# Hybrid layer on one core: the last row tile's turning spread over gate/up blocks, the third key product placed nearer, two first down splits swapped, an own buffer for first parts

## The chip, the core and the metric

The kernel runs on one core of a Trainium2 chip. The metric is the device time of one execution in microseconds. The core has a matrix engine (PE), a vector engine (DVE), a scalar engine (ACT), a general engine (POOL) and a queue that issues most transfers (SP). Each engine runs its instructions in the order in which the program lists them for it.

## The reference, cut

One layer of a hybrid encoder: a gated DeltaNet and a short gated convolution side by side, an output projection, then a SwiGLU feed-forward. The input is 2048 rows of a new stream and 8 x 16 rows of running streams, 1024 columns each: 17 tiles of 128 rows.

```python
h = rmsnorm(x, g1);  P = h @ w_in                  # 1024 -> 3592 columns
qkv = silu(causal_dwconv(P[..., :1536]));  q, k = l2norm(q), l2norm(k)
A = where(i > j, (k * beta) @ k.T * decay, 0)      # in chunks of 64 rows
sol = triangular_solve(I + A, [v * beta, k * beta * exp(g)])
...                                                # state update over the chunks -> o
x = x + rmsnorm(concat(o, conv_out) @ w_o)         # output projection
h = rmsnorm(x, g2)
f = (silu(h @ w_gate) * (h @ w_up)) @ w_down       # 1024 -> 2816 -> 1024
x = x + rmsnorm(f)
```

All of it is in float32. The kernel splits each operand into a rounded high part and a low part (the remainder) and uses three products: high x high, high x low and low x high.

## The kernel before

The work runs in four phases on one core.

**Phase 1** (`tile_hybrid_layer_kernel`, to about L1160) projects the input and runs the DeltaNet. The 17 row tiles are in five groups (`GROUPS`) of 4, 4, 3, 3 and 3 tiles. For each group 28 blocks of 24 projection matmuls (L327) are run, in three slots of 9, 9 and 6. The order of PE here is written out by hand. Everything else that PE does for the group is hung into the slots by `plan()`: `PLAN` lists for each group the slot of every step, among them `pairs` (28 in groups 2 to 4: the products of the keys with themselves, `pair_keys`, L615 to L620), `load` (`solve_load`, L629: packing the result for the triangular solve), `store` (`solve_store`, L657: transposing the solution, L660 and L661) and `levels` (from `level_a`, L664, PE uses the solution, L672). Between `load` and `store` the solve runs in four pieces on DVE (L653, L655). `pair_keys` takes a bank of the two-bank pool `psg` (tile name `gbank`), and DVE multiplies it by the decay into AU (L620), which frees the bank. The decay itself has been scaled on DVE just before (`decay_scale`, L603). With three tiles the first two key products stand at slot `pairs`, the third at `pairs` + 3.

**Phase 2** is the output projection (`o_tile`): 48 matmuls for each row tile, then squares, a factor, and the rows. `o_rows` (L1244) computes the next norm's factor, scales the rows by it (hx, L1250, DVE), transposes them (ht, L1252, DVE) and stores them as hTd (L1255). For the last of the 17 tiles this is put off: `omark["last"]` holds it, and it runs after the first block of phase 3 (L1564).

**Phase 3** is gate/up (`gate_up`, L1494): three groups of 6, 6 and 5 row tiles, 22 blocks f each, of 84 matmuls (L1473). A block multiplies by a scheme with seven products in place of eight, so sums and differences of weight blocks are formed on DVE and POOL (L1439 to L1449), and copies on ACT (L1505 to L1507) empty PE's banks. During a group the rows of the next one are loaded (`ffn_load`, L1352) by `LOADF` from f = 4 on, into the pool `fd`, which is opened after the pools of phase 2 are closed (L1565).

**Phase 4** is the down projection in five chunks of the 2816 columns. `down_pair` (L1717) does seven products for a pair of row tiles; `load_parts` (L1650) loads the parts in the pieces (0, 2), (2, 4) and (4, 7), or (0, 4) and (4, 7) for the first two pairs of a chunk (`duo`), into a ring of three buffers named ar. `split` (L1641) rounds a part on ACT (L1644) and subtracts on DVE or POOL (L1647). The first parts of the first chunk are prepared during phase 3. `finish` (L1681) squares, scales and stores the rows in the last chunk.

Outside PE's order in phase 1, a planner fixes the order of each engine's instructions when the program is built, from a simulated run; `tc.issue_after` ties an instruction behind another one.

Of the kernel before, what the change touches and what calls it, by code (L numbers as in the profile page):

```python
# [9 lines left out]
F32 = mybir.dt.float32  # L10
# [37 lines left out]
TURNS = ({"k": ((19,), (19,), (31,), (31,)), "q": ((43,), (43,), (55,), (55,)), "v": ((52,), (52,), (64,), (64,))},  # L48
# [50 lines left out]
def kernel(  # L99
# [67 lines left out]
    with ExitStack() as ph:  # L167
# [723 lines left out]
        def plan(g, nx, events):  # L891
# [13 lines left out]
            for i in range(n):  # L905
                at(mask + i, decay_mask, g, i)
                at(pairs + 3 * (i // 2) + i % 2 - 1, decay_scale, g, i)
                at(pairs + 3 * (i // 2), pair_keys, g, i)
                at((52, 42, 33)[min(gi, 2)] + 3 * (i // 2), pair_queries, g, i)
# [303 lines left out]
        def o_tile(t, loads=()):  # L1213
# [20 lines left out]
            for n in range(2):  # L1234
                c = slice(n * 512, (n + 1) * 512)
                V.scalar_tensor_tensor(pss[n], pss[n], r, gpost[:, c], op0=ALU.mult, op1=ALU.mult)
                omark["V"] = V.tensor_add(xt[:, c], xt[:, c], pss[n])
            nc.scalar.dma_start(out=x2d[t], in_=xt)
            if t + 1 < NT:
                o_rows(t, xt, ss)  # L1240
            else:
                omark["last"] = lambda: o_rows(t, xt, ss)

        def o_rows(t, xt, ss):  # L1244
            for n in range(2):
                omark["A"] = A.activation(ojunk, xt[:, n * 512:(n + 1) * 512], AF.Square, accum_out=ss[:, 2 + n:3 + n])
            V.tensor_add(ss[:, 2:3], ss[:, 2:3], ss[:, 3:4])
            r = rstd(op, ss[:, 2:3], 1, 1.0 / D, EPS, "oy")
            hx = op.tile([P, D], F32, tag="hx", name="hx") if t else spare[0]
            V.tensor_scalar_mul(hx, xt, r)  # L1250
            ht = op.tile([P, D], F32, tag="ht", name="ht") if t else spare[1]
            V.transpose(ht, hx)  # L1252
            gi, i = FPLACE[t]
            if gi:
                nc.scalar.dma_start(out=hTd[gi][4 * i:4 * i + 4].rearrange("b f c -> (b f) c"), in_=ht)  # L1255
            for b in range(0 if gi else 4):
                c = i * P + 32 * b
                nc.sync.dma_start(out=hTd[gi][:, c:c + 32].rearrange("(j f) c -> f j c", f=32),
                                    in_=ht[32 * b:32 * b + 32].rearrange("f (j c) -> f j c", c=32))
# [79 lines left out]
    with ExitStack() as ph:  # L1339
# [218 lines left out]
        for gi in range(len(FGROUPS)):  # L1558
            if gi:
                *_, hid = ffn_prep(gi, hs, t3)  # L1560
            for f in range(NF):
                gate_up(gi, f, hid, gu_start(gi, f, hid))
                if (gi, f) == (0, 0):
                    omark["last"]()  # L1564
                    ps_o.close()  # L1565
                    fd = side.enter_context(tc.tile_pool(name="fd", bufs=1, reuse_waits="tile", side="right"))
                if f == 0 and gi + 1 < len(FGROUPS):
                    hs = {}
                    hload, loaded = ffn_load(gi + 1, fd, hs), []
                if gi + 1 < len(FGROUPS):  # L1570
                    with tc.issue_after(gmark["A"].ins):
                        while loaded:
                            ffn_gain(hs, [loaded.pop()])
# [35 lines left out]
    with ExitStack() as ph:  # L1609
# [40 lines left out]
        def load_parts(src, lo, hi, front=False):  # L1650
            n = src.shape[-2] * P
            a = da.tile([P, 4 * MC * P // 2], F32, tag="ar", name="ar", bufs=3)
            a = a[:, :(hi - lo) * n].rearrange("p (i c) -> p i c", c=n)
# [63 lines left out]
        def down_pair(ch, u, last):  # L1717
# [33 lines left out]
            for i in (0, 1, 2, 3, 5, 4, 6) if final else range(7):  # L1751
                b, mid, dst = steps[i]
                b = bank(b)
                if i == 3 and len(parts) == 4:
                    parts += load_parts(src, 4, 7)
                e = V if i in ((0,) if end else (0, 3)) or (duo and not ch and len(ready) < 2) else G
                if end and i == (4 if duo else 0):
# [190 lines left out]
```

## Time and profile before

| | us |
|---|---|
| median of 3 runs | 2416.18 |
| lowest, highest | 2414.71, 2419.66 |
| the profiled execution | 2417.77 |
| its span | 2415.7 |
| PE busy | 2398.2 |
| DVE busy | 1614.9 |
| ACT busy | 1065.4 |
| POOL busy | 564.0 |

The span is the time from the first to the last instruction of the profiled execution. "PE busy" is the time in which at least one matmul is running; span less PE busy is the time that PE waits, at the start, at the end and in between. DVE, ACT and POOL work beside PE, so their time counts only where PE has to wait for them.

### The profile page before, as it was taken

Reading aid. Unit: us, or ns where it says so; the run is one execution under the profiler, and the core shown is the slowest. Engines: PE = TensorE matmul, PEld = TensorE weight load, DVE = VectorE, ACT = ScalarE, POOL = GpSimd, SP = SyncE. Lnnn points to the kernel's source line nnn. Section 1 sums busy time; section 2 is a strip of 40 time slices with the busy share of each in tenths; the row PEclk is TensorE's granted clock in tenths of the full one; section 3 lists DMA queues with packets and bytes.
Section 4 is the critical chain, followed back from the end, with each engine's and each line's share of the span. In section 5 each row is a group of like instructions: output and inputs, shape, how many; then the busy total and the mean of one; then the engine's idle time right before and its main releaser. Section 6 shows DMA issues by size and latency. Waiting matters only on the chain.

```text
span 2415.7 us, 39069 instructions
## 1 busy us (share of the span) xinstructions
PE 2398.2 (99%) x14202; PEld 2200.6 (91%) x14202; DVE 1614.9 (67%) x3062; ACT 1065.4 (44%) x2367; POOL 564.0 (23%) x671
## 2 busy tenths in 40 slices
PE   9999999999999999999999999999999999999998
PEld 7888889999999988899999999999999988888877
DVE  7875765756767466888788744456455555676787
ACT  6645545546444444544444423334333345333443
POOL 1211001001110000255555100000000035455663
PEclk9999999999999999999999999999999999999999
DMA  8774655766787677698898888888988844334376
GB/s 296 253 244 170 221 199 195 256 218 238 259 262 256 226 186 232 216 345 286 278 278 265 288 253 255 255 266 270 304 301 285 249 155 131 100 117 129 118 234 207
DMA packets 317064, 561.37 MB, mean 232 GB/s; under 512 B 95940, under 2 KB 198536, under 8 KB 299592
## 3 DMA queue, kind: packets, MB, share of 16 engines
q1 hardware_dynamic: 216864, 490.66, 61.3%
q10 hardware_dynamic: 99784, 67.17, 8.9%
q8 instruction: 112, 1.84, 0.3%
q0 software_dynamic: 224, 1.05, 0.1%
q14 instruction: 80, 0.66, 0.1%
HBM read 400.09 MB, written 158.70 MB: 231 GB/s over the span
## 4 chain that ended last, share of the span: by engine, by line
PE 91%; DVE 4%; ACT 2%; DMA 1%; issue 1%; POOL 1%; ACTq 0%; SPq 0%; POOLq 0%; DVEq 0%
PE fbank L1473 35%; PE dbank L327 25%; PE fbank L1664 17%; PE dbank L1227 4%; PE ftbank L1227 4%; PE gbank L619 1%; PE tbank L385 1%; PE gbank L790 1%; PE gbank L806 1%; PE obank L798 1%; PE gbank L812 1%; PE obank L820 1%; PE gbank L626 1%; PE gbank L723 0%; PE gbank L501 0%
## 5 line engine op out<-in xcount | busy, mean ns | idle before, releaser
L1473 PE MATMUL fbank<-xh,fw 128*128 128x384 f32 (+1 forms) x3696 | 898.0, 326 | 2.9 <-ACT m L1506 1.7
L1473 PEld LDWEIGHTS fbank<-xh,fw 128*128 128x128 f32 x3696 | 651.0, 188 | 5.0 <-ACT m L1505 2.8
L327 PE MATMUL dbank<-hi,w 128*128 128x384 f32 (+1 forms) x2224 | 651.1, 363 | 0.0
L1473 PE MATMUL fbank<-xl,fw 128*128 128x384 f32 (+1 forms) x1848 | 601.9, 326 | 0.0
L327 PEld LDWEIGHTS dbank<-hi,w 128*128 128x128 f32 x2224 | 410.0, 188 | 40.2 <-issue 3.6
L1664 PE MATMUL fbank<-dw,as 128*128 128x512 f32 x1785 | 416.0, 391 | 2.7 <-ACT as L1644 1.3
L1664 PEld LDWEIGHTS fbank<-dw,as 128*128 128x128 f32 x1785 | 334.6, 188 | 77.1 <-ACT as L1644 1.7
L327 PE MATMUL dbank<-lo,w 128*128 128x384 f32 (+1 forms) x1112 | 396.6, 357 | 0.0
L1473 PEld LDWEIGHTS fbank<-xl,fw 128*128 128x128 f32 x1848 | 346.9, 188 | 0.0
L327 PEld LDWEIGHTS dbank<-lo,w 128*128 128x128 f32 x1112 | 209.3, 188 | 15.3
L1647 POOL TENSOR_TENSOR as<-ar,as 128x256 fp32r<-128x256 f32 (+1 forms) x202 | 173.8, 869 | 182.1 <-ACT as L1644 176.5
L1644 ACT CAST as<-ar 128x256 fp32r<-128x256 f32 (+1 forms) x287 | 118.9, 427 | 200.4 <-PE fbank L1664 144.4
L1617 DVE TENSOR_TENSOR acc<-acc,fbank 128x512 f32<-128x512 f32 x219 | 148.1, 683 | 87.3 <-PE fbank L1664 69.5
L1312 POOL TENSOR_TENSOR dw<-dr,dw 128x512 fp32r<-128x512 f32 x48 | 67.6, 1415 | 514.1 <-ACT dw L1310 513.8
L1448 ACT CAST fw<-rg 128x512 fp32r<-128x512 f32 x124 | 77.2, 622 | 224.5 <-PE fbank L1473 127.4
L331 DVE SCALAR_TENSOR_TENSOR acc<-R,vec,acc 128x512 f32<-128x512 f32 (+2 forms) x180 | 120.9, 673 | 27.8 <-ACT acc L368 22.4
L1521 DVE TENSOR_TENSOR c<-u,fbank 128x384 f32<-128x384 f32 (+1 forms) x66 | 34.8, 528 | 98.2 <-PE fbank L1473 98.2
L1517 DVE TENSOR_TENSOR m<-m,m 128x384 f32<-128x384 f32 (+1 forms) x44 | 23.1, 525 | 79.9 <-ACT m L1507 79.8
L1524 ACT ACTIVATE c<-c 128x384 f32<-128x384 f32 (+1 forms) x66 | 33.4, 507 | 95.3 <-DVE c L1523 95.3
L1449 POOL TENSOR_TENSOR fw<-rg,fw 128x512 fp32r<-128x512 f32 x44 | 66.6, 1515 | 34.7 <-ACT fw L1448 32.8
L1519 ACT ACTIVATE m<-fbank 128x384 f32<-128x384 f32 (+1 forms) x66 | 31.2, 473 | 94.4 <-PE fbank L1473 73.7
L360 POOL COPY hist<-R 128x3 f32<-128x3 f32 x60 | 18.5, 308 | 216.4 <-ACT R L336 171.6
(409 smaller groups left out, 3562.5 us busy)
## 6 DMA issues: line engine op xcount, KB each, us to landing
w<-wsplit SPq DMA_DIRECT2D x105, 1024.0 KB, 5.1
fw<-fsplit SPq DMA_DIRECT2D x188, 512.0 KB, 4.8
fsplit<-fw SPq DMA_DIRECT2D x94, 512.0 KB, 4.2
partd<-pt ACTq DMA_DIRECT2D x86, 384.0 KB, 6.5
rg<-in_w_gu SPq DMA_DIRECT2D x62, 512.0 KB, 4.3
wsplit<-w SPq DMA_DIRECT2D x28, 1024.0 KB, 4.9
ar<-partd SPq DMA_DIRECT2D x43, 384.0 KB, 3.2
wr<-in_w_in SPq DMA_DIRECT2D x32, 512.0 KB, 6.4
```

The source lines that it names most:

```text
L327: T.matmul(ps[:, :c], l[:, k, :], r[k][:, :c], start=(k == 0 and r is hi and l is wh), stop=(k == KD - 1 and l is wl))
L331: r = V.scalar_tensor_tensor(acc, raw(d), w[:, d:d + 1], acc, op0=ALU.mult, op1=ALU.add)
L1227: T.matmul(pss[n], m_[:, j, :], w_[k][:, n * 512:(n + 1) * 512], start=(k == 0 and ci == 0), stop=(k == KD - 1 and ci == 2))
L1312: e.tensor_tensor(out=w[1], in0=v, in1=w[0].bitcast(F32), op=ALU.subtract)
L1448: A.copy(w[:, 0], v)
L1449: e.tensor_tensor(out=w[:, 1], in0=v, in1=w[:, 0].bitcast(F32), op=ALU.subtract)
L1473: T.matmul(ps, w_[:, c], b_[k][:, :hw], start=(first and k == 0 and ci == 0), stop=(k == KH - 1 and ci == 2), skip_group_check=not first)
L1521: V.tensor_add(c21, u2, b3)
L1617: mark_d["V"] = V.tensor_tensor(out=dst if out is None else out, in0=dst, in1=ps, op=ALU.add)
L1644: ins = mark_d["A"] = A.copy(a[:, 0, :n], v)
L1647: mark_d["V" if e is V else "G"] = e.tensor_tensor(out=a[:, 1, :n], in0=v, in1=a[:, 0, :n].bitcast(F32), op=ALU.subtract)
L1664: ins = T.matmul(ps, a[:, x_, q * P:(q + 1) * P], w[y_], start=(start and q == 0 and ci == 0), stop=(q == c - 1 and ci == 2), skip_group_c ...
```

## The change

Four places are changed.

1. `o_rows` of the last row tile becomes a generator that is run in three steps after the blocks f = 0, 1 and 2 of gate/up. The squares and the factor stay at f = 0. The scaling hx moves from DVE to ACT, behind the last silu of block 1. The transposition on DVE comes behind the last product of block 2, with the store. The pools of phase 2 are closed, and fd is opened, at f = 2 in place of f = 0.
2. In the groups with three tiles the third key product moves from slot `pairs` + 3 to `pairs` + 1, its decay scaling from `pairs` + 2 to `pairs`, and `load` and `store` by two slots, from 32 to 30 and from 47 to 45.
3. In the first chunk of the down projection two subtractions change engines: pair 0's third one goes from POOL to DVE, pair 1's second one from DVE to POOL.
4. `load_parts` puts the loads of (0, 2) into a buffer of their own, af, in the pool `dn`; the ring ar serves the rest.

```diff
--- before.py
+++ after.py
@@ -42,9 +42,9 @@
 LATE = (*SEQS[0][:2], 7, 11, 19, 23, 27)
 PLAN = {0: (14, 20, 22, 26, 32, 36, 40, 50, (67, 69, 71), 75),
         1: (16, 20, 23, 28, 26, 33, 38, 51, (56, 58, 60), 66),
-        2: (8, 14, 17, 22, 17, 28, 32, 47, (52, 55, 58), 63),
-        3: (8, 14, 17, 22, 17, 28, 32, 47, (53, 56, 59), 64),
-        4: (8, 14, 17, 22, 17, 28, 32, 47, (52, 55, 57), 62)}
+        2: (8, 14, 17, 22, 17, 28, 30, 45, (52, 55, 58), 63),
+        3: (8, 14, 17, 22, 17, 28, 30, 45, (53, 56, 59), 64),
+        4: (8, 14, 17, 22, 17, 28, 30, 45, (52, 55, 57), 62)}
 TURNS = ({"k": ((19,), (19,), (31,), (31,)), "q": ((43,), (43,), (55,), (55,)), "v": ((52,), (52,), (64,), (64,))},
          {"k": ((17,), (20,), (23,), (26,)), "v": ((55,), (55,), (61,), (61,)), "q": ((62, 64), (63, 65), (64, 66), (65, 67))},
          {"k": ((14,), (14,), (17,), (17,)), "v": ((46,), (46,), (52,), (52,)), "q": ((57, 59), (58, 60), (59, 61), (60, 62))})
@@ -904,8 +904,8 @@
             at(norms, key_norms, g)
             for i in range(n):
                 at(mask + i, decay_mask, g, i)
-                at(pairs + 3 * (i // 2) + i % 2 - 1, decay_scale, g, i)
-                at(pairs + 3 * (i // 2), pair_keys, g, i)
+                at(pairs + (3 if n == MAXT else 1) * (i // 2) + i % 2 - 1, decay_scale, g, i)
+                at(pairs + (3 if n == MAXT else 1) * (i // 2), pair_keys, g, i)
                 at((52, 42, 33)[min(gi, 2)] + 3 * (i // 2), pair_queries, g, i)
             if gi:
                 at(QSUM[min(gi, 2)], query_sums, g)
@@ -1236,10 +1236,12 @@
                 V.scalar_tensor_tensor(pss[n], pss[n], r, gpost[:, c], op0=ALU.mult, op1=ALU.mult)
                 omark["V"] = V.tensor_add(xt[:, c], xt[:, c], pss[n])
             nc.scalar.dma_start(out=x2d[t], in_=xt)
+            rows = o_rows(t, xt, ss)
             if t + 1 < NT:
-                o_rows(t, xt, ss)
+                for _ in rows:
+                    pass
             else:
-                omark["last"] = lambda: o_rows(t, xt, ss)
+                omark["last"] = rows
 
         def o_rows(t, xt, ss):
             for n in range(2):
@@ -1247,9 +1249,16 @@
             V.tensor_add(ss[:, 2:3], ss[:, 2:3], ss[:, 3:4])
             r = rstd(op, ss[:, 2:3], 1, 1.0 / D, EPS, "oy")
             hx = op.tile([P, D], F32, tag="hx", name="hx") if t else spare[0]
-            V.tensor_scalar_mul(hx, xt, r)
+            yield
+            if t + 1 < NT:
+                V.tensor_scalar_mul(hx, xt, r)
+            else:
+                with tc.issue_after(gmark["A"].ins):
+                    A.activation(hx, xt, AF.Copy, scale=r)
+            yield
             ht = op.tile([P, D], F32, tag="ht", name="ht") if t else spare[1]
-            V.transpose(ht, hx)
+            with ExitStack() if t + 1 < NT else tc.issue_after(gmark["V"].ins):
+                V.transpose(ht, hx)
             gi, i = FPLACE[t]
             if gi:
                 nc.scalar.dma_start(out=hTd[gi][4 * i:4 * i + 4].rearrange("b f c -> (b f) c"), in_=ht)
@@ -1560,16 +1569,17 @@
                 *_, hid = ffn_prep(gi, hs, t3)
             for f in range(NF):
                 gate_up(gi, f, hid, gu_start(gi, f, hid))
-                if (gi, f) == (0, 0):
-                    omark["last"]()
+                if not gi and f < 3:
+                    next(omark["last"], None)
+                if (gi, f) == (0, 2):
                     ps_o.close()
                     fd = side.enter_context(tc.tile_pool(name="fd", bufs=1, reuse_waits="tile", side="right"))
-                if f == 0 and gi + 1 < len(FGROUPS):
+                if f == 2 and gi + 1 < len(FGROUPS):
                     hs = {}
                     hload, loaded = ffn_load(gi + 1, fd, hs), []
                 if gi + 1 < len(FGROUPS):
                     with tc.issue_after(gmark["A"].ins):
-                        while loaded:
+                        while f > 2 and loaded:
                             ffn_gain(hs, [loaded.pop()])
                     for _ in range(LOADF.count(f)):
                         k = next(hload)
@@ -1649,7 +1659,8 @@
 
         def load_parts(src, lo, hi, front=False):
             n = src.shape[-2] * P
-            a = da.tile([P, 4 * MC * P // 2], F32, tag="ar", name="ar", bufs=3)
+            a = (da.tile([P, 4 * MC * P // 2], F32, tag="ar", name="ar", bufs=3) if hi > 2 else
+                 dn.tile([P, 2 * MC * P // 2], F32, tag="af", name="af"))
             a = a[:, :(hi - lo) * n].rearrange("p (i c) -> p i c", c=n)
             (nc.gpsimd if front else nc.sync).dma_start(out=a, in_=src[:, lo:hi].rearrange("p i q c -> p i (q c)"))
             return [a[:, i] for i in range(hi - lo)]
@@ -1753,7 +1764,7 @@
                 b = bank(b)
                 if i == 3 and len(parts) == 4:
                     parts += load_parts(src, 4, 7)
-                e = V if i in ((0,) if end else (0, 3)) or (duo and not ch and len(ready) < 2) else G
+                e = V if i in ((0,) if end else (0, 3)) or (duo and not ch and (i > 1 if len(ready) < 2 else i == 2)) else G
                 if end and i == (4 if duo else 0):
                     load2()
                 if end and i == (5 if duo else 3):
```

## Rows read from the trace of the kernel before

**Rows 1.** The page's first part: busy us, share of the span, instructions.

```profile
PE 2398.2 (99%) x14202; PEld 2200.6 (91%) x14202; DVE 1614.9 (67%) x3062; ACT 1065.4 (44%) x2367; POOL 564.0 (23%) x671
```

**Rows 2.** Windows: start:end, length, busy by engine, PEclk, DMA share, GB/s.

```profile
1049.32:1063.78 14.46, 12.74 (x74) 12.42 (x73) 13.87 (x15) 5.75 (x12) 10.30 (x8) 1.00 1.02 405
2400.00:2416.00 16.00, 8.07 (x36) 6.36 (x34) 11.18 (x19) 2.90 (x8) 1.54 (x2) 0.90 0.38 119
```

**Rows 3.** Waits of PE: who <- for whom, us, times, longest.

```profile
PE fbank L1473 <- ACT m L1506: 1.7, 1, 1.7
...
PE fbank L1664 <- ACT as L1644: 1.3, 1, 1.3
...
PE fbank L1664 <- DVE as L1647: 1.0, 1, 1.0
PE gbank L672 <- DVE utd L660: 0.9, 1, 0.9
```

**Rows 4.** Timeline of DVE, gate/up: start, us, operation, [idle before].

```profile
1052.07 1.50 DVE L1250 TENSOR_SCALAR hx<-xo,oyr 128x1024 f32<-128x1024 f32 x1
...
1056.62 1.23 DVE L1252 STREAM_TRANSPOSE ht<-hx 128x1024 f32<-128x1024 f32 x1
...
1061.13 0.54 DVE L1523 TENSOR_TENSOR c<-u,fbank 128x384 f32<-128x384 f32 x1
...
1090.61 0.99 DVE L1449 TENSOR_TENSOR fw<-sD,fw 128x512 fp32r<-128x512 f32 x1 [1.16 <-ACT fw L1448]
```

**Rows 5.** Timeline of ACT there; last, all 128x1024 casts: total us, mean ns.

```profile
1061.70 0.52 ACT L1524 ACTIVATE c<-c 128x384 f32<-128x384 f32 x1 [2.23 <-DVE c L1523]
...
1062.90 0.48 ACT L1506 COPY m<-fbank 128x384 f32<-128x384 f32 x1 [0.17 <-DVE a L1537]
...
1072.76 0.62 ACT L1448 CAST fw<-sD 128x512 fp32r<-128x512 f32 x1 [1.49 <-PE fbank L1473]
...
L306 ACT CAST w<-wr 128x1024 fp32r<-128x1024 f32 x32 | 33.7, 1052 | 24.3 <-PE dbank L327 13.5 <-DMA wr<-in_w_in 10.5
```

**Rows 6.** Timelines of PE and DVE around the key products of group 3.

```profile
595.58 1.05 PE L619 MATMUL gbank<-kT 128*128 128x128 f32 x8
...
590.52 1.90 DVE L603 TENSOR_TENSOR dt<-dt,c 128x512 f32<-128x512 f32 x3 [2.34 <-ACT dt L599]
592.34 1.28 DVE L620 TENSOR_TENSOR AU<-gbank,dt 128x512 f32<-128x512 f32 x2
```

**Rows 7.** Timeline of PE where it takes up the solution of group 3.

```profile
631.72 0.69 PE L672 MATMUL gbank<-utd,AU 32*32 32x32 f32 x32 [0.89 <-DVE utd L660]
632.34 0.45 PE L327 MATMUL dbank<-hi,w 128*128 128x384 f32 x1
```

**Rows 8.** Timelines of POOL and DVE at the start of chunk 0.

```profile
1953.20 0.96 POOL L1647 TENSOR_TENSOR as<-ar,as 128x256 fp32r<-128x256 f32 x1 [10.53 <-ACT as L1644]
...
1955.94 4.14 DVE L1647 TENSOR_TENSOR as<-ar,as 128x256 fp32r<-128x256 f32 x4
```

**Rows 9.** All of line L1647: duration in ns, min/median/max, by engine.

```profile
L1647 POOL TENSOR_TENSOR as<-ar,as x202: 725/740/1477, 1953.2 to 2396.7; 128x256 fp32r<-128x256 f32 x77, 128x384 fp32r<-128x384 f32 x24
...
L1647 DVE TENSOR_TENSOR as<-ar,as x85: 409/420/1518, 1955.9 to 2382.3; 128x256 fp32r<-128x256 f32 x75, 128x384 fp32r<-128x384 f32 x10
```

**Rows 10.** Last chunk: timelines of ACT, DVE, SP, PE; a chain piece.

```profile
2309.68 0.52 ACT L1644 CAST as<-ar 128x384 fp32r<-128x384 f32 x1 [2.51 <-DMA ar<-partd]
...
2310.81 0.70 DVE L1696 TENSOR_TENSOR fbank<-fbank,gpo 128x512 f32<-128x512 f32 x1 [2.03 <-ACT junkd L1693]
...
2268.47 28.55 SPq L1654 DMA_DIRECT2D ar<-partd  x5
...
2306.08 6.54 SPq L1654 DMA_DIRECT2D ar<-partd  x4
...
2303.85 10.09 PE L1664 MATMUL fbank<-dw,as 128*128 128x512 f32 x43 [0.51 <-POOL as L1647]
...
2270.97 6.41 DMA ar<-partd
```

## The prediction

> **What bounds the kernel now.** I read the page first: PE is busy 2398.2 us, 99% of the span [rows 1]. The matmuls set the time, and the change removes no matmul, so whatever it can win is idle time of PE: 2415.7 − 2398.2 = 17.5 us. Second, the windows: in the last 16.0 us PE works 8.07, at a granted clock of 0.90 where the other stretch shown has 1.00 [rows 2]. That is 7.9 of the 17.5 us, and it lies in a tail that the diff does not touch. What is left, 9.6 us with the start, is in the list of PE's waits [rows 3], and the places that the diff names have four of its entries, and a fifth wait that a timeline shows [rows 10]:
>
> - 1.7 us, L1473 behind ACT's copy L1506: in the second gate/up block, before the copy's end at 1063.38
> - 0.9 us, L672 behind DVE's L660, the transposed solution of group 3: before 631.72
> - 1.0 us, L1664 behind DVE's low part L1647: chunk 0
> - 1.3 us, L1664 behind ACT's cast L1644, and 0.5 us, L1664 behind POOL's low part L1647: last chunk
>
> They add up to 5.4 us, 0.22% of the time, and that is the most which the four parts together can give. Third, the order in time on each engine around these places says what each wait hangs on.
>
> **Part 1, the last row tile.** In the second block DVE is busy for 13.87 of 14.46 us and PE for 12.74 [rows 2]: here DVE is the bound. DVE runs the scaling hx (L1250) at 1052.07 for 1.50 us and the transposition (L1252) at 1056.62 for 1.23, and only at 1061.13 the sum L1523 [rows 4]. ACT's silu L1524 waits 2.23 us for that sum, and the copy L1506 that lets PE go on ends at 1062.90 + 0.48 = 1063.38 [rows 5]; PE, 1.7 us idle, wanted it at 1061.7. The two operations are 2.73 us of DVE's time ahead of L1523, some 2.6 without the overlap of neighbours, so the copy can end near 1060.8, 0.9 us before PE wants it. The gap of 1.7 goes whole; what is late next is the same copy, with 0.9 to spare. Added elsewhere: the scaling on ACT, one pass over 128x1024. A cast of that shape takes ACT 1.05 us; twice as long would be 2.1. It stands behind the silu of the second block, and ACT has 1.49 us without work before 1072.76 [rows 5], so 1.05 is hidden and 2.1 would push the casts behind it by 0.6. I take the cast's 1.05, the nearest row. The transposition now follows L1537 of the third block, where DVE has 1.16 us idle before 1090.61 [rows 4] and needs 1.23: 0.1 late, within a block that has idle time. Its store moves with it on ACT's queue; the rows of this tile are read by loads of the last group, a group of 22 blocks later. The pool that takes the place of hx and ht opens two blocks later, but its first loads stand at the block with f = 4 as before, and SP keeps its order there: nothing. I take −1.7, bounds −1.9 and 0.
>
> **Part 2, the third key product.** Groups 2 to 4 have three tiles each. PE now does two key products, then 24 projection matmuls (9 + 9 + 6), then the third. The change leaves 6 between. 74 matmuls of the same width, 384, take 12.74 us in the second gate/up block [rows 2], 0.172 each, so the third product is wanted 18 x 0.172 = 3.1 us earlier, in group 3 at 595.58 − 3.1 = 592.5 [rows 6]. The solve then starts up to 3.1 us earlier and, as the place of L672 stays, group 3's wait of 0.9 goes. Groups 2 and 4 have no such wait and gain nothing.
>
> But the third product needs a bank. The pool has two, and both are held by the first two products until DVE has multiplied them by the decay (L620). DVE runs all three decay scalings (L603) first and then the two L620, which together take 1.28 from 592.34 [rows 6]; the first ends at about 593.0, and with some 0.06 for the signal PE would wait 593.06 − 592.48 = 0.6 us. The pattern is the same in groups 2 and 4: 3 x 0.6 = 1.8. That is one bound; the other is 0, if DVE takes the first L620 ahead of the second or third scaling. Nothing in the diff asks for that order, so I take 1.8. What queues behind the waiting product is all of PE, projections that need nothing of it. That PE lets nothing past shows at 631.72: L672 starts after 0.89 us of waiting, and matmuls of L327, which don't need it, come at 632.34 [rows 7]. The Trainium skill ("PSUM — Partial Sum Buffer", Engine vs sequencer instructions) states it as a rule: matmuls start and complete in program order. The trace agrees here; by that rule the early product costs PE its whole wait, and if others could pass it part 2 would be worth −0.9. Net: −0.9 + 1.8 = +0.9, bounds −0.9 and +1.8.
>
> **Part 3, the swap in chunk 0.** DVE is held by the last gate/up block and starts the low part of pair 1's second product at 1955.94; PE waits 1.0 us for it. POOL took pair 0's third low part at 1953.20 after 10.53 us without work [rows 8]. Swapped, POOL does pair 1's from about 1953.2 in 0.96, at most 1.48, the longest such row [rows 9]: by 1954.7, well before PE wants it at about 1956.5. DVE does pair 0's from 1955.94 in 0.42 to 1.52 [rows 9], done by 1957.5 at the worst; it belongs to the next product, and one product is six matmuls, 1.4 us at the rate of 43 in 10.09 us [rows 10], so it is wanted at about 1957.8. Some 0.3 to spare. I take −1.0, bounds −1.0 and −0.5.
>
> **Part 4, the first parts' own buffer.** In the last chunk ACT's cast at 2309.68 waited 2.51 us for a load into ar; a square stands behind it on ACT and holds DVE's gain L1696 at 2310.81 for 2.03 us [rows 10], and from there come the factor and the scaling that give PE a bank. SP issued that load at 2306.08 [rows 10], when a buffer of the ring came free, and it landed 3.6 us later. The load before it, of a pair's first parts, was issued at 2268.47 + 28.55 − 0.3 = 2296.7 [rows 10] and took the buffer that came free then. With the first parts out of the ring that buffer goes to the load in question, 9 us earlier, and the 1.3 goes. The 0.5 hangs on a chain that starts with the load of 6.41 us from 2270.97 [rows 10]; the loads ahead of it find their buffers earlier too, by some 1.5 us. −1.3 − 0.5 = −1.8, bounds −1.8 and 0 (0 if loads behind the new single buffer, on the same queue, come as late as now).
>
> **Sum.** −1.7 + 0.9 − 1.0 − 1.8 = −3.6 us. The profiled execution took 2417.77 and its span 2415.7; the same −3.6 on the median is 2416.18 − 3.6 = 2412.6. A measurement of this kernel can tell about 0.2%, 4.8 us, from no change, so the forecast is "within".
>
> **The rivals.** First: the wait for the bank does not arise, because DVE takes the first L620 ahead of a scaling. For it: the order is planned anew, and PE's third product now hangs on that one operation. Against: group 3 as it stands [rows 6]. All five gaps go: 2416.18 − 5.4 = 2410.8, just beyond 0.2%. Second: the waits change their place. DVE is busy 96% of the second block [rows 2], and one low part takes it 0.41 or 1.52 us [rows 9], so a fresh order can bring the wait back one operation later. If parts 1 and 4 give nothing, −1.0 + 0.9 is left: 2416.1. Third, the slower side: the solve of groups 2 to 4 is a chain of small DVE operations that comes up to 3.1 us earlier, ahead of work that drains PE's projection banks. There are three such banks, so nothing waits until that work is two products late, 2 x 24 x 0.172 = 8.3 us; from there each us by which the chain pushes it stops PE, at most 3.1 − 0.6 = 2.5 in a group, 7.5 in three: 2412.6 + 7.5 = 2420.1. Against it: none of the waits in [rows 3] is one of L327.
>
> **How the numbers follow.** The forecast has 0.41, the first rival 0.28, the second 0.23, the third 0.08. Faster by over 0.2% is the first rival, 0.28; slower is the third with what lies beyond, 0.08; within, the rest, 0.64. The range takes in the first rival with half a microsecond for its roundings and the second with the upper bound of part 2 (+0.9 more): 2410.2 to 2417.1.
>
> **What would show it.** In the list of PE's waits: no L1473 behind L1506 (part 1); no L672 behind L660, but three new entries of L619 behind DVE's L620 of some 0.6 each (part 2); no L1664 behind DVE (part 3), and none behind ACT or POOL (part 4). PE's idle time falls from 17.5 to about 14. The forecast is wrong if L619 waits nowhere (then near 2410.8), if new waits stand in the first blocks of gate/up, or if L327 waits in groups 2 to 4.

## The result and the profile after

The changed kernel takes 2420.87 us (median of 18 runs, 2417.5 to 2425.59) against 2416.36 of the kernel before (18 runs, 2414.69 to 2419.66). The ratio is 1.0019, with a 95% interval of 1.0011 to 1.0026: 4.5 us slower, where 3.6 us less were forecast. The runs also lie further apart, over 8 us in place of 5. The profiled execution took 2422.64 us (span 2420.8). That is 1.8 above the median, so its rows show a little more loss than a usual run has.

Lines from 1239 on have moved by up to 11: L1506 is now L1515, L1507 is L1516, L1523 is L1532, L1524 is L1533, L1449 is L1458, L1647 is L1657, L1664 is L1675. The page's first part, as in [rows 1]:

```profile
PE 2401.8 (99%) x14202; PEld 2202.6 (91%) x14202; DVE 1613.1 (67%) x3061; ACT 1066.7 (44%) x2368; POOL 562.7 (23%) x671
```

PE is busy for 3.6 us more with the same 14202 matmuls: besides waiting longer, it must have run slower somewhere. Its idle time, span less busy, is 19.0 us where it was 17.5; about 14 was forecast. The list of PE's waits, as in [rows 3]:

```profile
PE fbank L1675 <- DVE accs L1627: 2.5, 1, 2.5
PE fbank L1482 <- ACT m L1516: 2.1, 1, 2.1
...
PE gbank L619 <- DVE AU L620: 1.4, 3, 0.6
PE fbank L1482 <- ACT m L1514: 0.9, 3, 0.6
PE fbank L1675 <- POOL as L1657: 0.5, 1, 0.5
...
PE fbank L1675 <- DVE dw L1321: 0.4, 1, 0.4
...
PE fbank L1675 <- ACT as L1654: 0.3, 1, 0.3
```

L672 behind L660 is gone, L1664 behind DVE's low part is gone, and the 1.3 behind ACT's cast in the last chunk is gone. Three waits of L619 have come, as forecast. The 0.5 behind POOL's low part in the last chunk stays, though part 4 was to take it away. Two long waits were not forecast: 2.1 us in the second gate/up block, and 2.5 us near the end. (The 0.4 behind DVE's dw and the 0.3 behind ACT's cast, both in the first chunk, are new too.) Windows around the two long ones (start:end, length, busy by engine, PEclk, DMA share, GB/s):

```profile
1058.70:1060.70 2.00, 2.00 (x12) 1.71 (x10) 2.00 (x3) 0.00 (x0) 1.49 (x1) 1.00 1.05 412
1062.80:1066.00 3.20, 3.20 (x10) 3.20 (x11) 1.78 (x4) 1.78 (x4) 2.21 (x2) 0.50 0.90 294
1068.00:1072.00 4.00, 4.00 (x25) 4.00 (x24) 3.90 (x7) 2.35 (x4) 1.13 (x1) 1.00 0.32 131
2390.00:2394.00 4.00, 4.00 (x18) 2.96 (x16) 1.86 (x4) 2.33 (x6) 2.15 (x3) 1.00 0.38 89
...
2398.00:2400.00 2.00, 2.00 (x6) 1.61 (x5) 0.04 (x1) 0.04 (x1) 0.69 (x1) 0.50 0.52 141
2402.00:2404.00 2.00, 2.00 (x11) 1.63 (x10) 2.00 (x5) 0.20 (x2) 0.63 (x2) 1.00 0.71 262
```

Behind each of the two waits PE runs at half its clock, 1.2 in place of 2.4 GHz: in 3.2 us it begins 10 matmuls where 18 fit, and it is back at 1.00 by 1068. At the full clock 10 take 1.7 us, so this stretch cost 1.5 us beside the wait. Behind the wait of 2.5 us some eight matmuls begin 0.43 us apart in place of 0.23, which is 1.6 us. Together the two stretches are 3.1 of the 3.6 us by which PE is busier. In the kernel before, the waits of 1.7 and 1.3 us had no such stretch behind them: the granted clock there was 1.00.

The second block, DVE, then POOL and ACT (start, us, operation, [idle before]), where [rows 4, 5] showed the one of before:

```profile
1054.27 1.50 DVE L1458 TENSOR_TENSOR fw<-sC,fw 128x512 fp32r<-128x512 f32 x1
1055.69 1.78 DVE L1451 TENSOR_TENSOR sD<-rg,sB 128x512 f32<-128x512 f32 x1
1057.39 1.65 DVE L1545 TENSOR_TENSOR a<-c,m 128x384 f32<-128x384 f32 x1
1058.96 1.78 DVE L1458 TENSOR_TENSOR fw<-sB,fw 128x512 fp32r<-128x512 f32 x1
...
1061.27 0.54 DVE L1532 TENSOR_TENSOR c<-u,fbank 128x384 f32<-128x384 f32 x1
...
1055.18 1.74 POOL L1458 TENSOR_TENSOR fw<-sA,fw 128x512 fp32r<-128x512 f32 x1
1056.88 1.74 POOL L1458 TENSOR_TENSOR fw<-rg,fw 128x512 fp32r<-128x512 f32 x1
1058.58 1.61 POOL L1458 TENSOR_TENSOR fw<-ru,fw 128x512 fp32r<-128x512 f32 x1
...
1061.84 0.52 ACT L1533 ACTIVATE c<-c 128x384 f32<-128x384 f32 x1 [5.49 <-DVE c L1532]
...
1062.27 0.46 ACT L1516 COPY m<-fbank 128x384 f32<-128x384 f32 x1
```

The scaling and the transposition are gone from here, yet L1532 stands where L1523 stood, with a block that begins 0.8 us later on DVE (its first sA is at 1052.24 in place of 1051.47). The operations that moved up run beside POOL's three subtractions, and each takes about as long as one of those. And ACT waits 5.49 us in front of the silu L1533, with the copy L1516 that PE wants queued behind it. It is another copy than the one of before: L1516 was L1507, and in the kernel before ACT made that copy ahead of the silu:

```profile
1058.99 0.48 ACT L1507 COPY m<-fbank 128x384 f32<-128x384 f32 x1
```

So in the change PE stops one product of 12 matmuls earlier in its order than before. The copy that it then waits for ends at 1062.73, where the one of before ended at 1063.38, and PE wanted it at 1060.7 in place of 1061.7.

The end of the last chunk, on SP in the kernel before and, with DVE and PE, in the changed one:

```profile
2373.19 0.43 SPq L1654 DMA_DIRECT2D ar<-lastd  x1
...
2376.98 1.13 SPq L1654 DMA_DIRECT2D ar<-partd  x2
```

```profile
2372.40 0.38 SPq L1665 DMA_DIRECT2D af<-lastd  x1
...
2379.75 0.55 DVE L1657 TENSOR_TENSOR as<-af,as 128x384 fp32r<-128x384 f32 x1
...
2385.10 0.57 SPq L1665 DMA_DIRECT2D af<-partd  x1
...
2396.47 6.24 PE L1675 MATMUL fbank<-dw,as 128*128 128x512 f32 x19 [2.46 <-DVE accs L1627]
```

Before, the last pair's first parts were loaded 4 to 5 us after the single's parts (lastd). Now both use the one buffer af, and the load comes 12.7 us behind. DVE reads the single's parts out of af until 2380.30; the other 4.8 us pass on SP's queue, behind loads and stores of rows that wait themselves.

### The profile page after: what moved, and what is told of

Same layout as the page of the kernel before. It is cut to its first block, busy times and chain, and to the rows that moved or that the text cites. A ratio compares the mean times of both kernels' runs of the same rounds, so it can differ in the third digit from the quotient of the medians.

```text
span 2420.8 us, 39066 instructions
## 1 busy us (share of the span) xinstructions
PE 2401.8 (99%) x14202; PEld 2202.6 (91%) x14202; DVE 1613.1 (67%) x3061; ACT 1066.7 (44%) x2368; POOL 562.7 (23%) x671
## 3 DMA queue, kind: packets, MB, share of 16 engines
q0 software_dynamic: 224, 1.05, 0.1%
## 4 chain that ended last, share of the span: by engine, by line
PE 90%; DVE 4%; DMA 3%; ACT 2%; issue 1%; POOL 1%; SPq 0%; ACTq 0%; POOLq 0%; DVEq 0%
PE fbank L1482 36%; PE dbank L327 24%; PE fbank L1675 16%; PE dbank L1227 4%; PE ftbank L1227 4%; PE tbank L385 1%; PE gbank L626 1%; DMA wr<-in_w_in 1%; PE gbank L790 1%; PE obank L798 1%; PE gbank L812 1%; PE gbank L806 1%; PE obank L820 1%; DMA af<-partd 0%; PE gbank L619 0%
## 5 line engine op out<-in xcount | busy, mean ns | idle before, releaser
L327 PE MATMUL dbank<-hi,w 128*128 128x384 f32 (+1 forms) x2224 | 650.9, 363 | 0.2 <-ACT w L1032 0.2
L327 PEld LDWEIGHTS dbank<-hi,w 128*128 128x128 f32 x2224 | 409.7, 188 | 40.2 <-issue 3.6
L1675 PE MATMUL fbank<-dw,as 128*128 128x512 f32 x1785 | 418.7, 392 | 3.7 <-DVE accs L1627 2.5
L1675 PEld LDWEIGHTS fbank<-dw,as 128*128 128x128 f32 x1785 | 335.6, 188 | 79.2 <-DVE accs L1627 2.9
L327 PE MATMUL dbank<-lo,w 128*128 128x384 f32 (+1 forms) x1112 | 396.6, 357 | 0.0
L327 PEld LDWEIGHTS dbank<-lo,w 128*128 128x128 f32 x1112 | 209.2, 188 | 15.7 <-DVE lo L242 0.2
L1657 POOL TENSOR_TENSOR as<-ar,as 128x256 fp32r<-128x256 f32 (+1 forms) x172 | 148.4, 873 | 113.9 <-ACT as L1654 98.2
L1654 ACT CAST as<-ar 128x256 fp32r<-128x256 f32 (+1 forms) x217 | 89.5, 427 | 136.1 <-PE fbank L1675 118.9
L1533 ACT ACTIVATE c<-c 128x384 f32<-128x384 f32 (+1 forms) x66 | 33.4, 506 | 94.3 <-DVE c L1532 94.3
L1458 POOL TENSOR_TENSOR fw<-rg,fw 128x512 fp32r<-128x512 f32 x44 | 66.6, 1515 | 33.5 <-ACT fw L1457 29.3
```

Of the source, the lines that this page charges most:

```text
L327: T.matmul(ps[:, :c], l[:, k, :], r[k][:, :c], start=(k == 0 and r is hi and l is wh), stop=(k == KD - 1 and l is wl))
L1458: e.tensor_tensor(out=w[:, 1], in0=v, in1=w[:, 0].bitcast(F32), op=ALU.subtract)
L1654: ins = mark_d["A"] = A.copy(a[:, 0, :n], v)
L1657: mark_d["V" if e is V else "G"] = e.tensor_tensor(out=a[:, 1, :n], in0=v, in1=a[:, 0, :n].bitcast(F32), op=ALU.subtract)
L1675: ins = T.matmul(ps, a[:, x_, q * P:(q + 1) * P], w[y_], start=(start and q == 0 and ci == 0), stop=(q == c - 1 and ci == 2), skip_group_c ...
```

## The experiments

All times are medians, with the kernel before measured beside each run on the same chip. The ratio is the one on record and can differ a little from that of the two medians (e2: 1.0008, by the medians 1.0011).

| run | us (range) | before | ratio (95%) |
|---|---|---|---|
| e1 part 1 | 2418.23 (2416.4 to 2421.7) | 2416.64 | 1.0008 (0.9999 to 1.0017) |
| e2 part 2 | 2419.24 (2417.9 to 2420.4) | 2416.64 | 1.0008 (0.9999 to 1.0017) |
| e3 part 3 | 2416.47 (2414.8 to 2418.2) | 2416.64 | 0.9998 (0.9989 to 1.0007) |
| e4 part 4 | 2418.26 (2415.2 to 2421.3) | 2416.64 | 1.0006 (0.9997 to 1.0015) |
| e5 no turning | 2416.69 (2414.5 to 2420.3) | 2416.76 | 0.9999 (0.9990 to 1.0008) |
| e6 single in ring | 2415.34 (2413.8 to 2416.9) | 2416.76 | 0.9993 (0.9984 to 1.0002) |
| e7 first multiply early | 2417.08 (2414.5 to 2419.6) | 2416.76 | 1.0001 (0.9992 to 1.0010) |
| e8 copy first | 2417.42 (2415.8 to 2420.6) | 2416.76 | 1.0004 (0.9995 to 1.0013) |
| e9 POOL reads nothing | 2412.69 (2411.7 to 2415.8) | 2416.55 | 0.9987 (0.9978 to 0.9996) |
| e10 parts 3, 4 | 2414.50 (2413.5 to 2417.2) | 2416.55 | 0.9991 (0.9983 to 1.0000) |
| e11 parts 2, 3, 4 | 2414.99 (2413.8 to 2416.2) | 2416.55 | 0.9994 (0.9986 to 1.0003) |
| e12 all, mended | 2416.04 (2413.7 to 2418.5) | 2416.55 | 0.9997 (0.9988 to 1.0006) |
| e13 POOL writes longer | 2412.63 (2410.9 to 2414.1) | 2416.49 | 0.9982 (0.9973 to 0.9991) |
| e14 part 1, lows on DVE | 2413.81 (2411.8 to 2416.3) | 2416.49 | 0.9988 (0.9980 to 0.9997) |
| e15 group on DVE | 2410.38 (2409.4 to 2411.2) | 2416.49 | 0.9975 (0.9964 to 0.9986) |
| e16 two blocks on DVE | 2411.25 (2410.8 to 2413.6) | 2416.49 | 0.9978 (0.9969 to 0.9987) |
| e17 part 2 on e15 | 2410.54 (2409.4 to 2412.0) | 2416.63 | 0.9975 (0.9966 to 0.9984) |
| e18 change, group on DVE | 2415.12 (2412.5 to 2418.4) | 2416.63 | 0.9995 (0.9986 to 1.0004) |

### Each part alone

Each of e1 to e4 has one part of the diff and nothing else of it.

> The change's part 1 alone (last row tile spread over blocks 0 to 2). Theory A (each part is worth the waits that it adds and removes at its own place, and a wait of PE of over 2 us also costs a stretch at half the granted clock behind it): the wait in the second gate/up block stays, now L1516's copy queued on ACT behind the silu, 2.0 to 2.1 us in place of 1.72, with some 1.5 us at a granted clock near 0.5 behind it, and some of the small waits of later blocks go: +0.9 us on the kernel before. Theory B (the planner's whole order changes with any edit, and the loss belongs to no one part): the wait at this place looks unlike that of the full change, and the total is anywhere from -2 to +5. My prediction's price for this part was -1.7.

> Part 2 alone (third key product nearer, load and store two slots earlier). Theory A: three waits of L619 behind DVE's L620, which move PE's later starts by 0.84, 0.65 and 0.85 us as in the full change, and L672's wait of 0.9 gone, with 0.4 gained at L501: +1.0 us. Theory B: other waits in groups 2 to 4 than in the full change. My prediction's price was +0.9.

> Part 3 alone (two low parts swapped in chunk 0). Theory A: the wait of 0.95 us before 1957.5 goes and nothing else changes, unless the two new waits of the full change in chunk 0 (0.4 behind DVE's dw, 0.3 behind ACT's cast) belong to this part: -1.0, or 0.0 with them. Theory B: waits elsewhere too.

> Part 4 alone (own buffer for first parts). Theory A: the wait of 1.3 us in the last chunk goes, and near the end a new wait of about 2.5 us stands at the single pair's last piece, because the load of the last pair's first parts now waits until the single's parts have left the one buffer (issue some 7 us later than in the kernel before); behind it 3 to 4 us at half the granted clock: -1.2 + 4.3 = +3.1 us, most of the whole loss. Theory B: no such wait without the other parts. My prediction's price was -1.8, bounds -1.8 and 0.

By the medians +1.6, +2.6, −0.2 and +1.6 us: 5.6 together, where the whole change has 4.5. No single part is clear of no change by its interval, so these four figures are no more than rough. What tells is the lists of waits: each part shows the new waits of its own place as in the whole change, which is theory A, and no new long wait of another part. A's prices were off: +0.9, +1.0 and +3.1 were expected of e1, e2 and e4. Part 1's wait behind L1516 is 2.0 us in the profile of e1; part 2's three waits of L619 are 1.4 in all; part 4's wait behind the single's last sum is 1.8. Two details differ. In the executions of e1 and e4, which have no part 2, L672 waits for nothing, and in e3 it waits 0.7: the 0.9 of [rows 3] is not there in each run. And the clock did not fall behind the waits of 2.0 (e1) and 1.8 (e4). The profiled execution of e1 is the fastest of its 11 (2416.41, median 2418.23), so this says nothing of the others. The window behind e1's wait:

```profile
1061.00:1063.50 2.50, 2.50 (x15) 2.50 (x16) 1.66 (x4) 1.07 (x3) 1.63 (x2) 1.00 0.84 287
```

Part 3 removes its wait, but other waits stand in the list of e3:

```profile
PE fbank L1664 <- ACT as L1644: 1.6, 1, 1.6
...
PE fbank L1664 <- DVE dw L1312: 0.4, 1, 0.4
```

The first, in the last chunk, was 1.3 before; the second, in the first chunk, is new.

### What the wait in the second block hangs on

e5 is part 1 with the last tile's scaling and transposition left out; the rows are stored unscaled and unturned (against e1, cut):

```diff
-                with tc.issue_after(gmark["A"].ins):
-                    A.activation(hx, xt, AF.Copy, scale=r)
+                hx = None
...
-            with ExitStack() if t + 1 < NT else tc.issue_after(gmark["V"].ins):
+            if hx is not None:
                 V.transpose(ht, hx)
```

> Part 1 with the last row tile's scaling and transposition left out altogether (its unscaled rows are stored in their place, so that tile is computed wrongly behind it). Theory A (the wait in the second block hangs on ACT's order, where the copy that PE wants stands behind the silu, and on DVE's pace beside POOL, not on the 2.7 us of the two operations): a wait of 1.5 us or more stays there, as in part 1 alone (2.0). Theory B (my prediction's: DVE's 2.7 us in that block are the cause): no wait of over 0.3 us in the second block, and about 2 us less than part 1 alone.

The wait is still there, the longest of all, with the half clock behind it:

```profile
PE fbank L1481 <- ACT m L1515: 2.3, 1, 2.3
```

```profile
1063.50:1066.00 2.50, 2.50 (x9) 2.50 (x9) 0.85 (x1) 0.49 (x1) 1.63 (x2) 0.50 1.04 391
```

So the 2.7 us of the two operations were not what PE waited for here. By its time e5 is less clear: −0.1 us against the kernel before is 1.7 under part 1's +1.6, close to the 2 us of theory B, though both runs spread over 5 us and more. In e5's list the smaller waits behind L1513 (L1514 in e1) are 0.7 in place of 1.5 us; the rest is open. e8 is part 1 with the silu put behind the copy on ACT (cut; put_off holds the silu of block 0's second half and its product):

```diff
+            if late:
+                with tc.issue_after(ins.ins):
+                    put_off.pop()()
+                s7 = ct("m7")
+                A.copy(s7, b3)
```

> Part 1 with one more edit: the silu of block 0's second half and the product that uses it are issued on ACT and DVE behind the copy of block 1's third bank, which PE wants. Theory A: the wait of 2.0 us behind that copy shrinks, and what is left is the wait for the next copy (behind DVE's product, about 0.6 us): some 1.4 us less than part 1 alone, and no stretch at half the clock in any of its executions. Theory B (DVE's pace alone decides): PE waits 1.5 us or more at the next copy.

The wait falls from 2.0 to 1.4 us and moves to the next copy, and further ones of up to 1.1 us come behind L1517 in later blocks. Against the kernel before it is +0.7 where part 1 alone is +1.6, so 0.9 is won of the 1.4 expected, by medians whose intervals are wider than that. A change of ACT's order thus moves the wait to another copy and does not remove it; the copy that is late now begins as DVE's product L1559 ends (1062.2). e9, e13 and e14, each on part 1, ask what slows DVE there. e9 lets POOL write zeros in place of its eight subtractions for blocks 2 and 3 (so these low parts are missing), e13 writes them three times (e13, cut; e9 has the memset once):

```diff
+                    if e is G and f in (2, 3):
+                        for _ in range(3):
+                            G.memset(w[:, 1].bitcast(F32), 0.0)
+                    else:
                         e.tensor_tensor(out=w[:, 1], in0=v, ...)
```

> Part 1 alone with POOL's low parts of blocks 2 and 3 left out: POOL writes zeros in their place (so these low parts of the weights are missing from the result), at the same place of its order, without reading anything. Theory A (in the second block DVE's two-input operations go only as fast as POOL's subtractions beside them, 1.65 to 1.78 us each in place of 0.55 to 0.68, and that is where the time taken from DVE went): between 1054 and 1060 DVE's sD, a and the low part of sB take 0.55 to 0.7 each, L1532 comes 3 us earlier, near 1057.5, and the wait of 2.0 us is gone. Theory B (DVE is slow there for another reason, or the wait hangs on ACT's order alone): the wait stays over 1 us.

> Part 1 with POOL writing the zeros three times in a row in place of each subtraction of blocks 2 and 3 (these low parts are missing from the result): 3 x 0.53 = 1.6 us an operation, about as long as the subtraction's 1.74, but it reads nothing. Theory A (POOL's reading holds DVE): DVE's two-input operations between 1050 and 1060 stay at 0.54 to 0.7 us beside the writes, no wait of over 0.5 us in the second block, within 1 us of the run with single writes (2412.7). Theory B (POOL's length or lateness counts): DVE's operations at 1.5 us or more, or a wait of over 1 us there.

e9 takes 2412.69, e13 2412.63: 3.9 us under the kernel before, where part 1 alone is 1.6 over it. Neither has a wait of gate/up in its list. e13, POOL and then DVE:

```profile
1053.22 3.33 POOL L1460 MEMSET fw<- 128x512 f32 x6
```

```profile
1053.75 0.55 DVE L1549 TENSOR_TENSOR a<-c,m 128x384 f32<-128x384 f32 x1
1054.22 0.68 DVE L1462 TENSOR_TENSOR fw<-sB,fw 128x512 fp32r<-128x512 f32 x1
1054.82 0.68 DVE L1449 TENSOR_TENSOR sA<-ru 128x512 f32<-128x512 f32 x1
1055.42 0.54 DVE L1536 TENSOR_TENSOR c<-u,fbank 128x384 f32<-128x384 f32 x1
```

POOL is busy without a break and DVE runs at 0.55 and 0.68 us beside it, where beside the subtractions the same operations take 1.65 and 1.78. From the block's first sA to L1536 (L1532 of the change) it is 5.85 us here, from 1049.57 to 1055.42, and 9.01 in e1. So it is not that POOL works or writes; it is that it reads beside DVE. Whether one operand would do the same was not tried: POOL's subtraction has two. e14 does all the work, with the subtractions of the two blocks on DVE:

```diff
-                    e.tensor_tensor(out=w[:, 1], in0=v, ...)
+                    (V if not gi and f in (2, 3) else e).tensor_tensor(out=w[:, 1], in0=v, ...)
```

> Part 1 with POOL's low parts of blocks 2 and 3 on DVE. Theory A (beside POOL's reading each two-input operation of DVE takes some 1.1 us more): DVE does three operations of 0.7 more in the second block, 2.1 us, and gets back 4 x 1.1 = 4.4: the wait of 2.0 falls below 0.5 and the time is 2 to 3 us under part 1 alone, 2415 to 2416. Theory B (DVE simply has too much work there): the wait grows beyond 2.5 us, and a stretch at half the clock stands behind it.

2413.81, 2.7 us under the kernel before and more than expected: the wait of 2.0 is gone, and no other one of gate/up is left. DVE does more operations in the block (two of the added ones at 1055.48 and 1057.16) and yet has L1532 at 1058.36, where e1 has it at 1059.35; from sC to L1532 it takes 7.64 us in place of 10.71:

```profile
1055.48 0.68 DVE L1458 TENSOR_TENSOR fw<-sA,fw 128x512 fp32r<-128x512 f32 x1
1056.09 0.55 DVE L1545 TENSOR_TENSOR a<-c,m 128x384 f32<-128x384 f32 x1
1056.56 0.68 DVE L1458 TENSOR_TENSOR fw<-sB,fw 128x512 fp32r<-128x512 f32 x1
1057.16 0.69 DVE L1458 TENSOR_TENSOR fw<-rg,fw 128x512 fp32r<-128x512 f32 x1
```

### What the waits of parts 2 and 4 hang on

e7 is part 2 with the second and third scalings tied behind the first multiply; e6 is part 4 with the single's parts kept in the ring (both cut; the comments are added):

```diff
+            with tc.issue_after(g["au0"].ins) if i and g["n"] < MAXT else ExitStack():
                 V.tensor_mul(dt, dt, bc(g["c2"][:, 4 * i:4 * i + 4]))
```

> Part 2 with the second and third decay scalings tied behind the first L620, so that the first bank comes free earlier. Theory A (the waits of L619 come from DVE's order: three scalings ahead of the first L620): no wait of L619, some 2.3 us less than part 2 alone (three places at 0.84, 0.65 and 0.85). Theory B (the product waits for something else, or the pushed-back scalings cost as much further on): a wait of L619 of 0.3 or more stays in each group, or a new one stands behind the second L620.

```diff
-            a1, a2 = load_parts(src, 0, 2)                # down_single
+            a1, a2 = load_parts(src, 0, 2, own=False)     # in the ring ar
```

> Part 4 with the single pair's first parts kept in the ring; only down_pair's loads of (0, 2) go to the own buffer. Theory A (the wait at the end comes from the single's parts, which hold the one buffer that the last pair's load needs): the wait of 1.8 us behind the single's last sum goes, the last pair's first load is issued at about 2378 again, and the wait of 1.3 in the last chunk stays gone: -1.2 us on the kernel before, some 3 under part 4 alone. Theory B (the wait comes from the planner's new order on SP in general): the wait stays between 1.5 and 2.5.

e7 has no wait of L619 left and is +0.3 us on the kernel before, where e2 is +2.6. DVE in group 3:

```profile
590.70 0.69 DVE L604 TENSOR_TENSOR dt<-dt,c 128x512 f32<-128x512 f32 x1 [2.25 <-ACT dt L599]
591.49 0.69 DVE L621 TENSOR_TENSOR AU<-gbank,dt 128x512 f32<-128x512 f32 x1
592.10 1.28 DVE L604 TENSOR_TENSOR dt<-dt,c 128x512 f32<-128x512 f32 x2
```

The first bank is free 0.8 us earlier than in [rows 6], and the waits go. e6 is −1.4 us, where e4 is +1.6. Its list has no wait behind the single's last sum and none behind ACT's cast in the last chunk; the 0.5 behind POOL's low part is still there. Both are theory A to within 0.2 us, by the medians.

### Together

> Part 3 and part 4 with the single's parts in the ring, without parts 1 and 2. Theory A (the parts add up): -0.2 of part 3 and -1.4 of this form of part 4: -1.6, some 2415.1. Theory B (the orders upset each other): within 0.5 of the kernel before.

> The same with part 2 whose first multiply by the decay comes ahead of the second scaling. Theory A: +0.3 on it, some 2415.4; no wait of L619 and no wait of L672. Theory B: part 2 so mended is worth the 0.9 of L672's wait: 2414.2.

> The whole change with two mends: the first multiply early in part 2, the single's parts in the ring in part 4. Part 1 as it is. Theory A (each part is worth what it showed alone): 2420.9 less 2.2 for the waits of L619, less 2.9 for the single buffer: 2415.8, or by the other sum, +1.6 +0.3 -0.2 -1.4 = +0.3 on the kernel before, 2417.0. So the loss of 4.5 is accounted for if it falls between these. Theory B: over 2419.

2414.50, 2414.99 and 2416.04. The last is the whole change with the two mends of e6 and e7. It is back at the kernel before, as the two sums of theory A had it (2415.8 and 2417.0), so the loss of 4.5 us is accounted for. The longest wait that remains from the change is part 1's of 2.0 us, with the half clock behind it. And the lists of e11, e12 and e17 have part 3's wait behind DVE's low part again, 0.7 us: its gain does not hold beside part 2 so mended.

e15 and e16 leave part 1 and part 2 out and move POOL's subtractions to DVE, in all 22 blocks of the first group or in two; e17 adds the mended part 2 to e15, e18 takes the change as given and moves the subtractions:

> Parts 3 and 4 (single's parts in the ring) with all of POOL's low parts of the first gate/up group on DVE. Theory A: the small waits of the first group behind L1505 and L1506 (2.6 us in all) mostly go: about 2412 to 2413. Theory B (DVE then has too much work, over 90% in the blocks): new waits in most of the 22 blocks and over 2420.

> The same with the low parts of blocks 2 and 3 alone on DVE. Theory A: the wait of 1.7 to 1.9 us in the second block goes: 2412.5 to 2413.5. Theory B: the wait stays or grows beyond 2 us: 2415 or more.

> Parts 3 and 4 (single's parts in the ring), part 2 with the first multiply early, and the first gate/up group's low parts on DVE. Theory A (places are independent): part 2 so mended was worth +0.3 to +0.5 beside other parts, so 2410.4 to 2410.9. Theory B (its gain, L672's wait of up to 0.9, shows where nothing else waits): 2409.5.

> The whole change as given, with the first gate/up group's low parts moved from POOL to DVE. Theory A: part 1's wait of 2.0 and its half clock go, with the small waits of the group, some 5.5 us under the change; the three waits of L619 and the wait behind the single's last sum (1.8 to 2.5 us) stay: 2420.9 - 5.5 = 2415.4. Theory B (the waits of parts 2 and 4 follow from the disorder ahead of them): they go too, 2411.

e15 is the fastest, 2410.38: 6.1 us under the kernel before, with an interval clear of no change. About 2.0 of them are parts 3 and 4 (e10), 4.1 the move to DVE. Its list of waits has no entry of L1473 any more. Most of the first group in one window, before and in e15:

```profile
1050.00:1350.00 300.00, 297.07 (x1705) 295.00 (x1704) 253.55 (x303) 128.71 (x258) 174.76 (x123) 1.00 0.88 285
```

```profile
1050.00:1350.00 300.00, 300.00 (x1732) 300.00 (x1732) 242.10 (x389) 140.42 (x268) 52.60 (x44) 1.00 0.89 293
```

DVE does 86 operations more and is busy for 11 us less, and PE waits for nothing there. e16 gets most of it from two blocks, 2411.25, more than expected. e17 adds nothing, 2410.54. e18 takes 2415.12, the 2415.4 of theory A. In its profiled execution the three waits of L619 stand, but the wait near the end is not there, though the last pair's load comes 11.9 us behind the single's; that execution is the fastest of its 11 (2412.5). So the late load need not stop PE, and how often it does in e18 stays open.

## Why the prediction was wrong

**What bounds the kernel** held: all that was lost is PE's time. But the sum priced a wait at its own length. In the profiled execution the waits of 2.1 and 2.5 us cost 3.6 and 4.1 with the slow stretches behind them. No row of before shows this price, since its longest wait was 1.7 us.

**Part 1** failed at the step "the two operations are 2.73 us of DVE's time ahead of L1523 ... so the copy can end near 1060.8". It took the durations of all other operations as given. [rows 9] showed already that one low part takes DVE 0.41 or 1.52 us, and I used that for a rival only. From the start of sA, the operation ahead of the scaling, to L1523 it was 1061.13 − 1051.47 = 9.66 us; in the change it is 1061.27 − 1052.24 = 9.03. Of 2.73 us only 0.63 arrived: sD, a and the low part of sB took 1.78, 1.65 and 1.78 in place of 0.65, 0.55 and 0.68, and of the rest mainly the second sA became shorter, 0.68 in place of 1.78. The scaling's own 1.50, beside POOL's L1517 and L1522, is twice the 0.75 that is the median of the 17 scalings of L1250; what made it longer was not tried. The transposition, which has one operand, ran beside POOL at 1.23, as in all 17 tiles; what moved up to stand there has two. The Trainium skill ("SBUF — State Buffer", Who interferes with whom) states that an operation of DVE with two inputs from SBUF, the memory that these tiles lie in, contends with one of POOL that reads it, not with one that only writes, and it calls the ports that the two share an exclusive lock. The trace agrees: 1.65 to 1.78 us beside POOL's subtractions in the change, 0.55 to 0.68 beside POOL's writes in e13. The second failure is the bound "−1.9 and 0", which has no place for a loss: with a fresh order on ACT, another copy, L1516, went behind the silu and was wanted one product earlier. The scaling on ACT was not at fault: it took 1.14 us at 1071.1, against the 1.05 of the sum.

**Part 2** was right in its mechanism, the bank, and in its sign; e2 measured more, +2.6 for +0.9. One wait, on PE in group 3 of the change:

```profile
592.90 0.34 PE L327 MATMUL dbank<-hi,w 128*128 128x384 f32 x1
593.69 1.16 PE L619 MATMUL gbank<-kT 128*128 128x128 f32 x8 [0.46 <-DVE AU L620]
```

From start to start it is 0.79 where 0.17 is usual: 0.62, the 0.6 of the sum; in groups 2 and 4 it is 0.53 and 0.74, so 1.9 in all for the 1.8. What failed is the gain of −0.9: L672's 0.9 was the price of one execution, absent in others with the same order ahead of it (e1, e4).

**Part 3**: the wait of 1.0 went, as forecast. By the medians −0.2 was left of −1.0 (e3); the interval, −2.7 to +1.7 us, allows either. The list of e3 has a new wait of 0.4 behind DVE's dw, for which the sum had no term, and a longer one in the last chunk.

**Part 4** was right on the 1.3, which went (e6: −1.4). Its −0.5 did not come: the wait behind POOL's low part in the last chunk is 0.5 in the change and in e6, and absent in e4 and e10; what it hangs on stays open. It failed above all at "bounds −1.8 and 0 (0 if loads behind the new single buffer ... come as late as now)". They come later than now: the last pair's load, issued 4 to 5 us after the single's in the kernel before, had to wait for the single's parts to leave the buffer and then for SP's queue, and PE waited 1.8 (e4) and 2.5 us (the change). I had read the buffer's use in the pairs only, not in `down_single`, which calls the same function.

**The rivals.** L619 did wait, so the first did not arise. The second is what happened to part 1, but with a price that it did not have. The third has the right side and the wrong place: L327 waits nowhere in groups 2 to 4. That its 2420.1 lies near the 2420.9 measured is luck.

## What to carry to other kernels

Taking an operation off a busy engine gives back its duration only if what moves up runs as fast as before: look beside which operation of the other engine it will now stand. A buffer taken out of a ring needs the list of everything that calls for it, with the two uses that lie closest. And where one engine's work is cheap alone and dear beside a neighbour, doing both on one engine can be the faster way, as in e14 and e15.

## What the runs showed of the hardware that was not expected

PE's clock: behind waits of 2.06, 2.46 (the change) and 2.33 us (e5) the granted clock was 0.50 for some 3 to 4 us, as the matmuls' starts show (0.32 us apart in place of 0.17). Behind 1.7, 1.8 and 1.9 us it stayed at 1.00. Behind 2.02 us it stayed (e1), behind 2.03 it fell (e12). What decides between these two is not shown. That fits the wider spread of the change's runs, with mean clocks of 0.998 in six of its 18, on average 2422.8 us, and 0.999 in twelve, 2420.1.

DVE beside POOL: an operation with two inputs of 128x512 takes DVE 0.68 us alone and up to 1.78 beside a subtraction of POOL; POOL's write of zeros over the same shape, repeated without a break for 3.3 us, did not lengthen such operations (0.68 us beside it).
